# Start order, early weights, rope on VectorE, turns between blocks, and tiles at multiples of 512 bytes in a hybrid S5 and attention layer

## The chip, the core and the metric

One core of a Trainium2 chip runs the whole layer. The core has five engines with queues of their own: TensorE (PE, matrix products and transposes), VectorE (DVE), ScalarE (ACT), GpSimd (POOL) and SyncE (SP, which here only issues DMAs). The metric is the device time of one execution in microseconds. All times below are of this core.

## The reference, cut to what matters

512 tokens of width 1024 pass one decoder layer. One projection of the normalised input feeds an S5 branch, a dilated attention branch and two gates.

```python
h = rms_norm(x, norm_w)
proj = h @ w_in
u_s, z_s, q, k, v, z_a, r_s, r_a = split(proj)

# S5 branch: diagonal complex state space in 4 chunks of 128 tokens
y_s = s5_branch(u_s, lam_re, lam_im, log_dt, b_re, b_im, c_re, c_im, d_skip, w_glu)
y_s = (y_s * silu(z_s)) @ w_ssm_out

# attention: 3 head groups (dilation 1, 4, 16), 8 heads of 64, window of 129 keys
q, k = rms_norm(q, q_norm_w), rms_norm(k, k_norm_w)
q, k = apply_partial_rope(q, positions), apply_partial_rope(k, positions)   # first 16 of 64
y_a = dilated_attention(q, k, v)     # softmax per group, groups merged by their sums
y_a = (y_a * silu(z_a)) @ w_attn_out

m = sigmoid(r_s) * y_s + sigmoid(r_a) * y_a
out = x + m @ w_o
```

All of it is float32. In `s5_branch` the complex recurrence `h[t] = a * h[t-1] + B u[t]` runs over 64 groups with 64 states, then `Re(C h) + D u`, GELU and a gated product with `w_glu`.

## The kernel before, in words

**Products.** Each large product is done as three products of a reduced float32 type: an operand is split in a high part (`hi`) and what is left (`lo`), and `hi*hi + lo*hi + hi*lo` is summed (`mm3`, line 63 is the helper that records every matmul, line 67 the one that records every transpose). So each weight tile of 128 x 1024 numbers is loaded by SP into `w_raw` (two buffers), its high part is made by ACT (`w_hi`, L116) and its low part by DVE (`w_lo`, L118); for the first two weights by POOL, since `lo_w` holds `pool` at the start. There are three buffers each of `w_hi` and `w_lo`, and weights are fetched two ahead of their use (`look`).

**Order.** The program is written as one stream of stages; a scheduler with a model of the engines sets the order of each engine's queue. `tc.issue_after(ins)` makes what is written inside it stand behind the instruction `ins` on its engine. Between the stages, units of the large projection are put as fillers.

**Stages.** (1) x comes in four blocks of 128 tokens (`x_t[0..3]`, tile `x_all`); ACT sums the squares (L240), DVE works out the reciprocal root by integer and Newton steps (L123 to L128, L242), DVE and ACT scale a block each (L248, L246), TensorE transposes (`hps`), ACT and DVE make `hT_hi` (L259) and `hT_lo` (L260). This is done in two halves of 256 tokens. (2) Eight u units (`u_unit`): the first three by halves, so that they begin when the first half of hT is there; each one's result `uT` goes to DRAM and comes back in another layout (`ud`, `sza`, `uss`). Beside them DVE works out the tables of S5 (L348 to L417 and L460 to L463) and rope's sine and cosine. (3) `W` and `xps` (inputs of the scan; the coefficients come from `coef`, L285 to L287), then the scan itself on DVE (L647 to L652, written into `Xs`), with projection units as fillers on TensorE. (4) y units (`yps`), GELU, the gated product, the output of the S5 branch. (5) Four attention blocks `hp = 0..3` of two heads per group.

**An attention block.** `qk_first` and `qk_second` project q, k and v with tokens on partitions ("TOK" products: 128 x 512, weights high and low against hT). `qk_norm` scales them (L858) and applies rope on POOL (L864 to L869: four operations on the first 16 of each 64 columns of `qraw`). `qk_turn` transposes them (`qtp`) and copies them with the norm weights as a factor (`wcol`; ACT L885, DVE L886) into `qkp`. The scores go to `sps`, DVE masks them (L941), ACT takes the exponential into `Pt` (L943), DVE and POOL work out the merged denominators (L978 to L986, sums per token moved by POOL in `sfb`, L990) and DVE scales `Pt` (L997). `values` transposes `Pt` (`ptp`), copies it (`ptb`; ACT L1039, DVE L1041) and multiplies by `V` into `ot`. A block's values are computed within the next block's projection, ahead of the last of `qk_second`'s four weights (`mid`, with `kq == 3`), and the scheduler may move them; `v0_unit` projects the V of group 0 with a bank of the pool `pj`.

Of the kernel before, what the change touches and what calls it, by code (L numbers as in the profile page):

```python
# [13 lines left out]
I32 = mybir.dt.int32  # L14
# [38 lines left out]
def tile_hybrid_block(ctx: ExitStack, tc: tile.TileContext, x, positions, norm_w, w_in, lam_re, lam_im,  # L53
# [83 lines left out]
    lo_w = [dve]  # L137
# [55 lines left out]
    def load_w(srcs, kts, cols):  # L193
        raw = wp.tile([P, kts, cols], F32, name="w_raw", tag="w_raw", bufs=2)
        w = cols // len(srcs)
        for i, s in enumerate(srcs):
            sp.dma_start(raw[:, :, i * w:(i + 1) * w], s.rearrange("(k p) c -> p k c", p=P))
# [39 lines left out]
    junk = big.tile([P, D], F32, name="junk", tag="s6a")  # L237
    for h in range(2):
        for r in (2 * h, 2 * h + 1):
            act.activation(junk, x_t[r], AF.Square, accum_out=ss[:, r:r + 1])  # L240
# [3 lines left out]
        for r in (2 * h, 2 * h + 1):  # L244
            if r % 2:
                act.activation(x_t[r], x_t[r], AF.Copy, scale=rst[:, r:r + 1])  # L246
            else:
                dve.tensor_scalar(x_t[r], x_t[r], rst[:, r:r + 1], None, op0=ALU.mult)  # L248
        for q in range(KT // 2):
# [18 lines left out]
    Xs = big.tile([P, 2, G // 2, NI, NJ], F32, name="Xs", tag="s2")  # L268
    Xsv = Xs.rearrange("p a g i j -> p a g (i j)")

    def load_u(j, Uj=None):
# [3 lines left out]
        return Uj.rearrange("p (g c) -> p g c", g=8)  # L275

    def coef(dst, p0, a1, a2, n0, n1, t, eng):
# [9 lines left out]
        dve.tensor_tensor(dst, dst, tv, op=ALU.add)  # L287
# [37 lines left out]

    first = [(get_w(), pj_tile()) for _ in range(3)]
# [7 lines left out]
    lr = scr([G, N])  # L334
    li = scr([G, N])
    dt = scr([G, 1])
    sp.dma_start(lr, lam_re[0])
    sp.dma_start(li, lam_im[0])
    sp.dma_start(dt, log_dt.rearrange("o g -> g o"))
# [36 lines left out]
    dte = scr([G, 1])  # L376
    exp_exact(dte, dt, [G, 1], "ea")
# [86 lines left out]
    act.activation(BB[:, 0], BB[:, 2], AF.Copy, scale=-1.0)  # L464

# [9 lines left out]
    for j in range(3, 8):  # L475
        u_unit(j)
        for i in {3: (0, 1, 2), 4: (3,)}.get(j, ()):
            early[i] = load_u(i, sza[:, i])
# [73 lines left out]
    qkw = scr([P, 2, NG, HD])  # L552
    sp.dma_start(qkw[:, 0].rearrange("p g d -> p (g d)"),
                 q_norm_w[0].rearrange("g d -> (g d)").unsqueeze(0).to_broadcast([P, NG * HD]))
    sp.dma_start(qkw[:, 1].rearrange("p g d -> p (g d)"),
                 k_norm_w[0].rearrange("g d -> (g d)").unsqueeze(0).to_broadcast([P, NG * HD]))
    dve.tensor_scalar(qkw[:, 0], qkw[:, 0], -0.125, None, op0=ALU.mult)
    wps = bank("wcp")
    for g in range(NG):
        for a in range(2):  # L560
            wd = sml.tile([1, 2, HD], F32, name="wd", bufs=2)
            pool.tensor_copy(wd, qkw[0:1, a, g].unsqueeze(1).broadcast_to([1, 2, HD]))
            pe.matmul(wps[:, 2 * g + a:2 * g + a + 1], wd.rearrange("p a d -> p (a d)"), ident[0:1, 0:1],
                      start=True, stop=True, skip_group_check=True)
    dve.tensor_copy(wcol.rearrange("p g a -> p (g a)"), wps[:, 0:6])
    pool.memset(wcol[0:16], 1.0)
    pool.memset(wcol[64:80], 1.0)

    tC = cst.tile([P, NG, NB, 2, 16], F32, name="tC")
    tS = cst.tile([P, NG, NB, 2, 16], F32, name="tS")  # L570
    for g in range(NG):
        for a in range(2):
# [618 lines left out]
```

## Time and profile before

| | |
|---|---|
| median of 3 runs | 720.77 us (719.61 to 723.12) |
| profiled execution | 722.95 us |
| its span (first to last instruction) | 721.2 us |
| TensorE busy | 689.3 us (96%), 4789 instructions |
| DVE busy | 460.8 us (64%) |
| ACT busy | 314.8 us (44%) |
| POOL busy | 179.8 us (25%) |
| DMA | 82.14 MB, 114 GB/s mean |

A row of the waits names the engine and line that stood idle, what released it, the total, the number of times and the longest. A row of the timeline gives start, duration, engine, line, operation, what it writes and reads, its shape, and in brackets the idle time before it with what ended it. A row of the stretches gives each engine's busy time (and count) in a stretch, then the granted clock of TensorE as a share of full speed, the share of DMA time and GB/s.

### The profile page before, as it was taken

How to read it: one execution, taken by the hardware profiler on the slowest of the kernel's cores; microseconds unless marked ns; L12 is line 12 of the kernel's file. 1: busy time of each engine (PE TensorE's matmuls, PEld its weight loads, DVE VectorE, ACT ScalarE, POOL GpSimd, SP SyncE). 2: the span in 40 equal slices, each digit the busy share in tenths (PEclk: the TensorE clock that was granted, in tenths of full speed). 3: DMA queues.
4: the chain of work that ended last, by engine and by line, in shares of the span. 5: the costliest groups of instructions: out<-in, count | busy, mean ns of one | idle time of the engine just before them, and what ended most of it. 6: DMA issues, size and time to landing. Idle time of an engine off the chain costs nothing.

```text
span 721.2 us, 12599 instructions
## 1 busy us (share of the span) xinstructions
PE 689.3 (96%) x4789; PEld 571.6 (79%) x4789; DVE 460.8 (64%) x928; ACT 314.8 (44%) x631; POOL 179.8 (25%) x330
## 2 busy tenths in 40 slices
PE   2799899999999999999999999999989998999997
PEld 2697677788977888888889888788868887888886
DVE  6766865999969544674325659756764667364832
ACT  6433544423247653342144456537253734543320
POOL 3421020630316502640000326121601251220000
PEclk9989999999999999999999999999999999999999
DMA  8425742564537635555333432312312221327341
GB/s 206 107 62 149 181 108 66 131 165 153 118 86 157 150 90 161 153 163 181 104 89 100 132 88 61 87 50 69 97 50 71 77 88 30 117 75 252 128 145 59
DMA packets 137213, 82.14 MB, mean 114 GB/s; under 512 B 32696, under 2 KB 125632, under 8 KB 137024
## 3 DMA queue, kind: packets, MB, share of 16 engines
q1 hardware_dynamic: 135088, 78.96, 38.0%
q0 software_dynamic: 2048, 2.36, 2.3%
q8 instruction: 38, 0.62, 0.4%
q14 instruction: 23, 0.19, 0.1%
q10 hardware_dynamic: 16, 0.00, 0.0%
HBM read 68.46 MB, written 10.49 MB: 109 GB/s over the span
## 4 chain that ended last, share of the span: by engine, by line
PE 87%; ACT 4%; DMA 4%; SPq 2%; DVE 2%; issue 0%; ACTq 0%
PE pj L63 72%; DMA w_raw<-in_w_in_dram 4%; PE yps L63 3%; PE sps L63 3%; PE ot L63 2%; PE ptp L67 2%; PE xps L63 1%; PE kps L63 1%; ACT w_hi L116 1%; PE qtp L67 1%; SPq L454 1%; PE wps L67 1%; ACT qkp L885 1%; PE yT L67 1%; SPq L227 1%; ACT ptb L1039 1%
## 5 line engine op out<-in xcount | busy, mean ns | idle before, releaser
L116 ACT ACTIVATE w_hi<-w_raw 128x1024 fp32r<-128x1024 f32 x100 | 106.2, 1063 | 230.2 <-PE pj L63 196.7
L118 DVE TENSOR_TENSOR w_lo<-w_raw,w_hi 128x1024 fp32r<-128x1024 f32 x98 | 124.4, 1269 | 102.0 <-ACT w_hi L116 97.2
L63 PE MATMUL pj<-hT_lo,w_hi 128*128 128x512 f32 (+1 forms) x344 | 132.2, 385 | 3.6 <-DVE hT_lo L260 3.6
L63 PE MATMUL pj<-hT_hi,w_hi 128*128 128x512 f32 (+1 forms) x344 | 132.9, 389 | 2.7 <-ACT V L917 1.4
L63 PE MATMUL pj<-hT_hi,w_lo 128*128 128x512 f32 (+1 forms) x344 | 131.6, 384 | 1.6 <-DVE w_lo L118 1.6
L63 PE MATMUL pj<-w_hi,hT_hi 128*128 128x512 f32 (+1 forms) x288 | 106.5, 370 | 0.0
L63 PE MATMUL pj<-w_lo,hT_hi 128*128 128x512 f32 (+1 forms) x288 | 105.7, 367 | 0.0
L63 PE MATMUL pj<-w_hi,hT_lo 128*128 128x512 f32 (+1 forms) x288 | 105.3, 369 | 0.0
L63 PEld LDWEIGHTS pj<-hT_lo,w_hi 128*128 128x128 f32 x344 | 66.7, 194 | 16.0 <-DVE hT_lo L260 4.6
L63 PEld LDWEIGHTS pj<-hT_hi,w_hi 128*128 128x128 f32 x344 | 66.1, 193 | 15.4 <-ACT V L917 2.1
L63 PEld LDWEIGHTS pj<-hT_hi,w_lo 128*128 128x128 f32 x344 | 66.5, 193 | 14.5 <-DVE w_lo L118 2.7
L63 PEld LDWEIGHTS pj<-w_hi,hT_hi 128*128 128x128 f32 x288 | 54.4, 189 | 8.6 <-DVE Xs L651 0.2
L63 PEld LDWEIGHTS pj<-w_hi,hT_lo 128*128 128x128 f32 x288 | 54.4, 189 | 8.5
L63 PEld LDWEIGHTS pj<-w_lo,hT_hi 128*128 128x128 f32 x288 | 54.4, 189 | 8.4
L886 DVE SCALAR_TENSOR_TENSOR qkp<-qtp,wcol,qkp 128x512 fp32r<-128x512 f32 (+1 forms) x32 | 23.2, 747 | 26.9 <-ACT qkp L885 26.4
L943 ACT ACTIVATE Pt<-Pt,st 128x256 f32<-128x256 f32 (+1 forms) x64 | 31.0, 493 | 14.1 <-DVE st L941 14.0
L747 POOL TENSOR_TENSOR kt<-kt,dg 16x128 f32<-16x128 f32 x8 | 12.0, 1505 | 92.0 <-ACT kt L746 86.0
L864 POOL TENSOR_TENSOR rt<-qraw,tC 128x256 f32<-128x256 f32 x12 | 14.0, 1170 | 84.0 <-DVE qraw L858 83.7
L751 POOL DMA_DIRECT2D dd<-kt x64 | 33.7, 535 | 2.4 <-POOL kt L747 2.4
L885 ACT ACTIVATE qkp<-qtp,wcol 128x512 fp32r<-128x512 f32 (+1 forms) x32 | 21.2, 688 | 21.8 <-PE qtp L67 16.1
L973 POOL COPY sw<-st 32x4 f32<-32x4 f32 x64 | 11.9, 187 | 69.8 <-ACT Pt L943 67.0
L990 POOL COPY sfb<-sd 32x2 f32<-32x2 f32 x64 | 18.0, 282 | 27.9 <-DVE sd L986 25.1
(265 smaller groups left out, 1271.8 us busy)
## 6 DMA issues: line engine op xcount, KB each, us to landing
w_raw<-in_w_in_dram SPq DMA_DIRECT2D x40, 512.0 KB
w_raw<-in_w_in_dram SPq DMA_DIRECT2D x112, 128.0 KB
w_raw<-in_w_glu_dram SPq DMA_DIRECT2D x8, 512.0 KB
w_raw<-in_w_ssm_out_dram SPq DMA_DIRECT2D x8, 512.0 KB
w_raw<-in_w_o_dram SPq DMA_DIRECT2D x8, 512.0 KB
x_all<-in_x_dram SPq DMA_DIRECT2D x4, 512.0 KB
ud<-uT SPq DMA_DIRECT2D x8, 256.0 KB
uss<-ud SPq DMA_DIRECT2D x8, 256.0 KB
```

Of the source, the lines that this page charges most:

```text
L63: last[0] = nc.tensor.matmul(*a, **k)
L67: last[0] = nc.tensor.transpose(*a, **k)
L116: act.activation(hi, src, AF.Copy, scale=scale)
L118: e.tensor_tensor(lo, src, hi.bitcast(F32), op=ALU.subtract)
L747: pool.tensor_tensor(kt[:, :, T - 1, :], kt[:, :, T - 1, :], dg, op=ALU.add)
L751: pool.dma_start(M[Q * t:Q * t + Q, :, 0:P - Q * t], kt[:, :, t:].rearrange("q g k p -> q g (k p)"))
L864: pool.tensor_tensor(t1, rh[:, :, :, 0:16], cv.broadcast_to([P, NB * 2, 2, 16]), op=ALU.mult)
L885: act.activation(hi, ps[sl], AF.Copy, scale=w)
L886: dve.scalar_tensor_tensor(lo, ps[sl], w, hi.bitcast(F32), op0=ALU.mult, op1=ALU.subtract)
L943: act.activation(o, o, AF.Exp, bias=nm, scale=-1.0, accum_out=st[:, kind, 1, h, b:b + 1])
L973: pool.tensor_copy(sw[32 * r:32 * r + 32, :, :, b], st[32 * b:32 * b + 32, 1, :, :, r])
L990: pool.tensor_copy(fb[32 * b:32 * b + 32, :, r], d[32 * r:32 * r + 32, 1, :, b])
```

## The change: what it does

- **Tiles at multiples of 512 bytes.** A tile `room` of 320 bytes per partition goes in ahead of `hT_hi`; the large tiles began at 192 modulo 512, now they begin at 0. The small `wd` tiles are gone (below).
- **First low parts on DVE.** `load_w` is split in `fetch_w` (the DMA) and the split into parts; DVE makes all low parts.
- **ScalarE's order at the start is fixed** by `last_act`: Square 0 and 1, `w_hi` of weight 0, Square 2, scaling, seven `hT_hi`, `w_hi` of weight 1, the eighth, `w_hi` of weight 2, Square 3, and so on. The three small DMAs of lambda and dt go to ACT's queue, at the start.
- **Weights into Xs.** `w_early` holds four weights in the region in which `Xs` is set up later (behind the fourth u unit). Weights 2 to 5 are fetched there right behind x; weights 6 and 7 go to the two raw buffers.
- **Tables behind hT.** S5's table work on DVE stands behind the second half's scaling and hT (`behind_h`); the scan's tables behind the coefficients; rope's tables behind the W units. `wcol` comes from one transpose instead of six small products.
- **Rope on DVE** for all groups of all blocks.
- **Turns between blocks of six products**: the four turns of a block's first two groups are put one each ahead of four token blocks of `qk_second` and tied there. `values` is put behind the token block (2, 1) of the weights for `hp == 0`, behind (1, 3) else. All `ptb` copies are ACT's, except in the last block. The V of group 0 gets a bank of its own (`v0p`).

```diff
+    room = cst.tile([P, 80], F32, name="room")
+    pool.memset(room[:, 0:1], 0.0)
...
-    def load_w(srcs, kts, cols):
-        raw = wp.tile([P, kts, cols], F32, name="w_raw", tag="w_raw", bufs=2)
+    def fetch_w(i, raw=None):
+        srcs, kts, cols = plan[i]
+        if raw is None:
+            raw = wp.tile([P, kts, cols], F32, name="w_raw", tag="w_raw", bufs=2)
...
+    def load_w(i, hi_behind=None, lo_behind=None):
+        if i not in raws_in:
+            fetch_w(i)
+        raw = raws_in.pop(i)
...
-        split(hi, lo, raw, lo_eng=lo_w[0])
+        with queued_after(hi_behind):
+            last_act[0] = act.activation(hi, raw, AF.Copy).ins
+        with queued_after(lo_behind):
+            dve.tensor_tensor(lo, raw, hi.bitcast(F32), op=ALU.subtract)
...
-    lo_w[0] = pool
+    w_early = big.tile([P, 4, KT, P], F32, name="w_early", tag="s2")
     for r in range(NB):
         sp.dma_start(x_t[r], xv[r])
         if r in (1, 2):
-            prefetch(len(loaded) + 1)
-    lo_w[0] = dve
+            fetch_w(r - 1)
+    fetch_w(2, w_early[:, 0])
...
+        if h:
+            loaded.append(load_w(2, last_act[0], lo_done))
+            square(3)
...
+        if h == 0:
+            loaded.append(load_w(0, last_act[0], scaled))
+            square(2)
...
+            if h == 0 and q == 2:
+                loaded.append(load_w(1, hi_done, lo_done))
...
+    for i in range(3):
+        fetch_w(3 + i, w_early[:, 1 + i])
     first = [(get_w(), pj_tile()) for _ in range(3)]
...
+    behind_h = ExitStack()
+    behind_h.enter_context(tc.issue_after(scaled))
+    behind_h.enter_context(tc.issue_after(hi_done))
...
+    def tables_last():
+        with tc.issue_after(coefs[0]):
+            scan_tables()
...
+    with tc.issue_after(coefs[0]):
+        pos_i = scr([P, NB], I32)
...
+        pe.transpose(wps[:, 0:2 * NG], wq, ident[:2 * NG, :2 * NG])
...
-            pool.tensor_tensor(t1, rh[:, :, :, 0:16], cv.broadcast_to([P, NB * 2, 2, 16]), op=ALU.mult)
+            dve.tensor_tensor(t1, rh[:, :, :, 0:16], cv.broadcast_to([P, NB * 2, 2, 16]), op=ALU.mult)
...
-                    if h == 0:
+                    if h == 0 or hp < NP - 1:
                         act.copy(pt[:, k0 * P:], ps[:, k0 * P:])
...
-            def mid(kq):
-                if kq == 1:
-                    qk_turn(0, raws[0], *QK)
-                if kq == 2:
-                    with queued():
-                        qk_turn(1, raws[1], *QK)
-                if kq == 3:
-                    values(hp, Pt, V)
+            steps = {(2, 3): (0, 0), (3, 0): (0, 1), (3, 1): (1, 0), (3, 2): (1, 1)}
+
+            def mid(kq, r):
+                if (kq, r) not in steps:
+                    return False
+                g, a = steps[kq, r]
+                with queued():
+                    qk_turn(g, raws[g], *QK, turned=(a,))
+                return True
+
+            def after(kq, r):
+                if (kq, r) == ((2, 1) if hp == 0 else (1, 3)):
+                    values(hp, Pt, V)
...
-            finv = v0_unit(hp + 1, V)
+            finv = v0_unit(hp + 1, V, bank("v0p"))
```

ACT's queue at the start, before (`junk` is the output of Square, `x_all` a scaling, `hT_hi` a high part of h, the `L371` and `L372` rows are of the tables):

```order
3 L240 ACTIVATE junk,scr<-x_all 128x1024 x2
4 L116 ACTIVATE w_hi<-w_raw 128x1024
5 L240 ACTIVATE junk,scr<-x_all 128x1024
6 L246 ACTIVATE x_all<-x_all,scr 128x1024
7 L116 ACTIVATE w_hi<-w_raw 128x1024
8 L240 ACTIVATE junk,scr<-x_all 128x1024
9 L259 ACTIVATE hT_hi<-hps,nwc 128x256 x8
10 L116 ACTIVATE w_hi<-w_raw 128x1024
11 L246 ACTIVATE x_all<-x_all,scr 128x1024
12 L371 ACT_TABLE_LOAD
13 L371 ACTIVATE scr<-scr 128x32
14 L372 ACTIVATE scr<-scr 128x32
```

The second weight's high part and the fourth Square stand ahead of the first `hT_hi`, and a table load with two sines ahead of the second half's. Now:

```order
7 L215 ACTIVATE w_hi<-w_raw 128x1024
8 L266 ACTIVATE junk,scr<-x_all 128x1024
9 L283 ACTIVATE x_all<-x_all,scr 128x1024
10 L294 ACTIVATE hT_hi<-hps,nwc 128x256 x7
11 L215 ACTIVATE w_hi<-w_raw 128x1024
12 L294 ACTIVATE hT_hi<-hps,nwc 128x256
13 L215 ACTIVATE w_hi<-w_early 128x1024
14 L266 ACTIVATE junk,scr<-x_all 128x1024
15 L283 ACTIVATE x_all<-x_all,scr 128x1024
16 L294 ACTIVATE hT_hi<-hps,nwc 128x256 x8
17 L215 ACTIVATE w_hi<-w_early 128x1024
18 L331 COPY uT<-pj 128x4x8x8x2
```

Seven of the first half's pieces come right behind the scaling, the second weight behind the seventh; the third weight is in `w_early`, and the tables' work stands behind the first `uT`.

TensorE's queue in the projection of block 2, where the values of block 1 are computed, before (`pj` is the TOK product, `ptp` a transpose of `Pt`, `ot` the product with V, `qtp` a turn):

```order
2025 L67 MATMUL qtp<-ident,qraw 128x128 x4
2026 L63 MATMUL pj<-w_hi,hT_lo 128x512
2027 L63 MATMUL pj<-w_hi,hT_hi 128x512
2028 L63 MATMUL pj<-w_lo,hT_hi 128x512
2029 L63 MATMUL pj<-w_hi,hT_lo 128x512
2030 L67 MATMUL qtp<-ident,qraw 128x128 x4
2031 L67 MATMUL ptp<-ident,Pt 128x128 x10
2032 L63 MATMUL ot<-ptb,V 64x4x32 x6
2033 L67 MATMUL ptp<-ident,Pt 128x128 x20
2034 L63 MATMUL ot<-ptb,V 64x4x32 x8
2035 L63 MATMUL ot<-ptb,V 64x128 x16
```

All 30 transposes and 30 products with V stand together at the end of the projection. Now:

```order
2006 L63 MATMUL pj<-w_hi,hT_lo 128x512
2007 L67 MATMUL ptp<-ident,Pt 128x128 x4
2008 L63 MATMUL ot<-ptb,V 64x4x32 x6
2009 L67 MATMUL ptp<-ident,Pt 128x128 x8
2010 L63 MATMUL ot<-ptb,V 64x4x32 x8
2011 L67 MATMUL ptp<-ident,Pt 128x128 x8
2012 L63 MATMUL ot<-ptb,V 64x128 x8
2013 L67 MATMUL qtp<-ident,qraw 128x4x32 x4
2014 L63 MATMUL pj<-w_hi,hT_hi 128x512
2015 L63 MATMUL pj<-w_lo,hT_hi 128x512
2016 L63 MATMUL pj<-w_hi,hT_lo 128x512
```

Ten transposes stand 18 products ahead of the first row (46 behind the scores), the rest alternate with the products with V, and turns of four come behind, with six TOK products between two of them.

The same place for block 0's values, now (before, the first six `ptp` stood 62 TOK products behind the scores):

```order
1763 L63 MATMUL pj<-w_hi,hT_lo 128x512
1764 L67 MATMUL ptp<-ident,Pt 128x128 x8
1765 L63 MATMUL ot<-ptb,V 64x4x32
1766 L67 MATMUL ptp<-ident,Pt 128x128 x8
1767 L63 MATMUL ot<-ptb,V 64x4x32 x5
1768 L67 MATMUL ptp<-ident,Pt 128x128 x2
1769 L63 MATMUL ot<-ptb,V 64x4x32
1770 L67 MATMUL ptp<-ident,Pt 128x128 x4
1771 L63 MATMUL ot<-ptb,V 64x4x32 x7
1772 L67 MATMUL ptp<-ident,Pt 128x128 x8
1773 L63 MATMUL ot<-ptb,V 64x128 x8
1774 L67 MATMUL qtp<-ident,qraw 128x4x32 x4
```

Twenty-one TOK products stand between the last scores and the first of these transposes, and no TOK product stands among them.

More of the change, by code (lines that the diff above doesn't have):

```diff
@@ L1 @@
 import math
-from contextlib import ExitStack
+from contextlib import ExitStack, nullcontext
 import numpy as np
@@ L237, in tile_hybrid_block, with square @@
     junk = big.tile([P, D], F32, name="junk", tag="s6a")
+    def square(r):
+        with queued_after(last_act[0]):
+            last_act[0] = act.activation(junk, x_t[r], AF.Square, accum_out=ss[:, r:r + 1]).ins
+    square(0)
+    square(1)
     for h in range(2):
-        for r in (2 * h, 2 * h + 1):
-            act.activation(junk, x_t[r], AF.Square, accum_out=ss[:, r:r + 1])
+        if h:
+            loaded.append(load_w(2, last_act[0], lo_done))
+            square(3)
         w = slice(2 * h, 2 * h + 2)
@@ L243, in tile_hybrid_block @@
         rsqrt(rst[:, w], ms[:, w], [P, 2], ra_[:, w], rb_[:, w])
[L244 to L248, printed above, removed]
+        scaled = dve.tensor_scalar(x_t[2 * h], x_t[2 * h], rst[:, 2 * h:2 * h + 1], None, op0=ALU.mult).ins
+        if h == 0:
+            loaded.append(load_w(0, last_act[0], scaled))
+            square(2)
+        with queued_after(last_act[0]):
+            r = 2 * h + 1
+            act.activation(x_t[r], x_t[r], AF.Copy, scale=rst[:, r:r + 1])
         for q in range(KT // 2):
@@ L333, in tile_hybrid_block @@
         u_unit(j, first[j][1])
[L334 to L339, printed above, removed]
+    for j in range(3):
+        early[j] = load_u(j, sza[:, j])
     def exp_exact(dst, src, shape, pfx):
@@ L476, in tile_hybrid_block @@
         u_unit(j)
[L477 to L478 removed]
+        if j == 3:
+            Xs = big.tile([P, 2, G // 2, NI, NJ], F32, name="Xs", tag="s2")
+            Xsv = Xs.rearrange("p a g i j -> p a g (i j)")
+        if j == 4:
+            early[3] = load_u(3, sza[:, 3])
         wx(*((), (), (0,), (1,), (2, 3))[j - 3])
@@ L549, in tile_hybrid_block @@
     maskB_f = maskB.rearrange("p a k -> p (a k)")
[L552 to L572, printed above, removed]
-            w1 = qkw[:, a, g, 0:8].unsqueeze(1).broadcast_to([P, NB, 8])
-            w2 = qkw[:, a, g, 8:16].unsqueeze(1).broadcast_to([P, NB, 8])
-            pool.tensor_tensor(tC[:, g, :, a, 0:8], rcos, w1, op=ALU.mult)
-            pool.tensor_tensor(tC[:, g, :, a, 8:16], rcos, w2, op=ALU.mult)
-            pool.tensor_tensor(tS[:, g, :, a, 0:8], rsin, w2, op=ALU.mult)
-            pool.tensor_tensor(tS[:, g, :, a, 8:16], rsin, w1, op=ALU.mult)
-    pool.tensor_scalar(tS[:, :, :, :, 0:8], tS[:, :, :, :, 0:8], -1.0, None, op0=ALU.mult)
     def tok_granule():
@@ L594, in tok_granule, with v0_unit @@
         return pss
-    def v0_unit(hp, V):
-        ps = cm_unit(hT_hi, hT_lo)
+    def v0_unit(hp, V, ps=None):
+        ps = cm_unit(hT_hi, hT_lo, ps=ps)
         vt = t2k("vt")
@@ L906, in qk_first, with qk_second @@
         return raws
-    def qk_second(hp, mid=None):
-        pss = wide_granule(hT_hi, hT_lo, mid)
+    def qk_second(hp, mid, after):
+        pss = wide_granule(hT_hi, hT_lo, mid, after)
         raw = new_raw(0)
```

111 lines of the change are left out of this document (75 added, 36 removed).

## The prediction

> **What bounds the kernel now.** The page's busy times come first, then the waits of TensorE, then its busy time by stretch.
>
> ```profile
> PE 689.3 (96%) x4789; PEld 571.6 (79%) x4789; DVE 460.8 (64%) x928; ACT 314.8 (44%) x631; POOL 179.8 (25%) x330
> ```
> ```profile
> PE hps L67 <- DVE x_all L248: 10.2, 1, 10.2
> PE ptp L67 <- ACT ptb L1039: 3.5, 6, 0.8
> PE xps L63 <- ACT W L307: 3.1, 1, 3.1
> ```
> ```profile
> 0.00:18.00 18.00, 5.22 (x25) 4.86 (x25) 11.60 (x45) 11.14 (x18) 6.87 (x13) 1.00 0.87 206
> 18.00:36.00 18.00, 13.02 (x96) 11.58 (x95) 14.20 (x74) 8.60 (x18) 7.96 (x29) 0.96 0.43 108
> 36.00:54.00 18.00, 18.00 (x158) 16.48 (x158) 10.93 (x31) 5.51 (x7) 3.92 (x2) 0.85 0.27 61
> 54.00:72.00 18.00, 16.64 (x74) 12.67 (x73) 12.23 (x23) 5.68 (x7) 3.07 (x4) 1.00 0.57 148
> 72.00:90.00 18.00, 14.76 (x124) 12.18 (x123) 14.95 (x31) 10.46 (x21) 0.00 (x0) 0.91 0.71 182
> 90.00:126.00 36.00, 36.00 (x350) 28.02 (x350) 22.51 (x34) 15.73 (x45) 5.35 (x7) 1.00 0.32 87
> 126.00:200.00 74.00, 74.00 (x499) 61.83 (x498) 69.36 (x100) 25.43 (x43) 25.03 (x30) 1.00 0.53 139
> ...
> 440.00:455.00 15.00, 15.00 (x79) 12.33 (x78) 14.40 (x39) 7.45 (x17) 10.74 (x24) 1.00 0.24 70
> 512.00:540.00 28.00, 25.53 (x175) 20.84 (x174) 18.16 (x30) 12.29 (x25) 8.71 (x9) 1.00 0.27 76
> ```
>
> Columns behind the stretch: its length, then busy time of PE, weight loads, DVE, ACT and POOL, the granted clock, DMA share, GB/s. TensorE is the bound, 689.3 us of a span of 721.2, so a saving counts only if it removes matmul time or fills one of its 32 us of holes. Of these 22.7 lie before 90 us (12.8, 5.0, 1.4 and 3.2 by the rows), about 2.5 in each of two attention blocks, and the tail after 702 us is not touched. To them comes the lower clock of 0.96, 0.85 and 0.91, which stretches matmuls without showing as a hole: 18 x (0.04 + 0.15 + 0.09) = 5.0 us. DVE is full beside a full TensorE in 126 to 200 (the scan) and in 440 to 455 (the first block's softmax): work added there can become a wait.
>
> **Start: low parts on DVE, ScalarE's order, four weights fetched early.**
>
> ```profile
> 9.07 2.34 POOL L118 TENSOR_TENSOR w_lo<-w_raw,w_hi 128x1024 fp32r<-128x1024 f32 x1 [6.37 <-ACT w_hi L116]
> ...
> 8.99 0.16 DVE L128 SCALAR_TENSOR_TENSOR scr<-scr 128x2 f32<-128x2 f32 x1
> 9.19 2.23 DVE L126 TENSOR_TENSOR scr<-scr 128x2 f32<-128x2 f32 x1
> 11.85 0.75 DVE L248 TENSOR_SCALAR x_all<-x_all,scr 128x1024 f32<-128x1024 f32 x1
> ...
> 9.31 1.06 ACT L240 ACTIVATE junk<-x_all 128x1024 f32<-128x1024 f32 x1 [0.32 <-DMA x_all<-in_x_dram]
> 11.85 1.15 ACT L246 ACTIVATE x_all<-x_all,scr 128x1024 f32<-128x1024 f32 x1 [1.40 <-DVE scr L128]
> 23.54 1.06 ACT L116 ACTIVATE w_hi<-w_raw 128x1024 fp32r<-128x1024 f32 x1 [3.98 <-DMA w_raw<-in_w_in_dram]
> 26.75 1.15 ACT L246 ACTIVATE x_all<-x_all,scr 128x1024 f32<-128x1024 f32 x1 [2.16 <-DVE scr L128]
> ...
> 12.66 3.67 PE L67 MATMUL hps<-ident,x_all 128*128 128x128 f32 x16 [10.15 <-DVE x_all L248]
> 15.99 0.77 PE L63 MATMUL pj<-hT_hi,w_hi 128*128 128x256 f32 x2
> ```
>
> The reciprocal root's tiny steps take 0.16 us each, but the one that starts at 9.19 takes 2.23: it ends with the POOL subtraction that began at 9.07. With the low part on DVE, behind the scaling of x0, it costs 0.2, so x0 is scaled from 9.8 (11.85 less 2.05). ScalarE scales x1 after its third Square (9.31 + 1.2), 10.5 to 11.6. The transposes that need x1 run from 11.6 instead of 13.0, and with 16 at 0.22 us the first product starts at about 14.8 instead of 15.99.
>
> "SBUF — State Buffer" in the Trainium skill (section "SBUF: two separate sides") calls the port pair of VectorE and GpSimd an exclusive lock: a VectorE operation with two SBUF inputs blocks fully against a GpSimd operation that reads SBUF. By that rule, the trace agrees: 2.23 us for a step of 0.16. [...]
>
> The first half's 72 products of 256 columns then take 8.6 us at 0.12 (the rows on the pace below), with one more for a clock not yet up (an allowance): end 24.7. The third weight, whose high part came at 23.54 because its DMA waited for a raw buffer, now lies in the region of Xs behind x3, and is split right after the first hT (about 17 to 19), before its unit is due at 20.6. The second half's x was scaled at 26.75, because DVE and ScalarE had let S5's table work run between; in the new order fourth Square, root (12 x 0.2) and scaling follow by 22.6, so transposes come right behind the first half, hT's eight pieces pace until 29, and 72 products end near 36.0.
>
> ```profile
> 45.33 0.28 PE L63 MATMUL pj<-hT_hi,w_lo 128*128 128x256 f32 x1
> ```
>
> It was 45.3, part of it the clock of 0.85, which came behind the holes of 24 to 36. Term: **-9.3**, from -7.3 (the clock falls again) to -10.6.
>
> **45 to 90 us: weights held by two raw buffers, ScalarE queued behind them.**
>
> ```profile
> 65.92 1.06 ACT L116 ACTIVATE w_hi<-w_raw 128x1024 fp32r<-128x1024 f32 x1 [5.63 <-DMA w_raw<-in_w_in_dram]
> 75.07 1.06 ACT L116 ACTIVATE w_hi<-w_raw 128x1024 fp32r<-128x1024 f32 x1 [5.50 <-DMA w_raw<-in_w_in_dram]
> 76.88 1.11 ACT L307 COPY W<-wps 128x512 f32<-128x512 f32 x2
> ```
>
> ScalarE stood 5.5 us and more at a high part whose DMA was late; behind it in its queue are the copies of uT and of W, and for W TensorE waited the 3.1 us above. With weights 2 to 5 already there, and 6 and 7 in the raw buffers, the eight u units never wait for a load. The stretch 54 to 90 holds 4.6 us of holes and 18 x 0.09 = 1.6 of clock: 6.2. Against it: S5's table work on DVE now starts behind the second half's hT, near 24 instead of 13, and W needs its result. Some 20 us of such small operations plus four low parts end near 52, and the first W is asked for after the sixth unit, near 53. Two more table loads of ScalarE lie under matmuls. I take 1.6 us of new waits (from 0 to 4, the next stall of the old size). Term: **-4.6**, from -2 to -6.2.
>
> **Scan and tables.** Rope's tables leave the start for the end of the W units.
>
> ```profile
> 29.52 0.24 POOL L577 TENSOR_TENSOR tS<-scr 128x32 f32<-128x32 f32 x1 [3.37 <-ACT scr L371]
> ...
> 198.18 0.69 DVE L652 TENSOR_TENSOR Xs<-Xs,scn 128x512 f32<-128x512 f32 x1
> ...
> 204.11 1.10 PE L63 MATMUL yps<-ab,Xs 64*64 64x64 f32 x60
> ```
>
> DVE finished the scan 5.2 us before TensorE read Xs (198.18 + 0.69 against 204.11). A dozen coefficient steps now stand ahead of the scan instead of between its steps, which adds nothing; new ahead of Xs are some 38 small steps of rope's and the scan's tables at 0.16 to 0.2, 6 to 8 us, and POOL's 24 table products (0.24 us each, the first in the rows) can each hold a DVE step up, 6 more: 6 to 14. The order gives TensorE 65 instead of 19 products between the last other work and that read, 46 x 0.228 = 10.5 us more cover. With 5.2 + 10.5 of cover against them: **0**, from 0 to +3 (a unit behind it that waits for its coefficients).
>
> **Attention: values among the TOK products, rope on DVE.**
>
> ```profile
> 500.25 1.32 PE L63 MATMUL sps<-qkp 64*128 64x256 f32 x12
> ...
> 527.29 0.66 PE L67 MATMUL ptp<-ident,Pt 128*128 128x128 f32 x4 [0.78 <-ACT ptb L1039]
> 536.12 0.50 PE L63 MATMUL pj<-hT_hi,w_hi 128*128 128x512 f32 x1 [0.46 <-ACT V L917]
> ...
> 506.62 2.06 DVE L997 TENSOR_SCALAR Pt<-Pt,sd 128x128 f32<-128x128 f32 x8
> ...
> 506.86 5.08 POOL L990 COPY sfb<-sd 32x2 f32<-32x2 f32 x15
> ```
> ```profile
> L416 DVE TENSOR_TENSOR pw<-pw,tq x3: 210/274/409, 38.0 to 44.7; 64x64 f32<-64x64 f32 x1, 64x128 f32<-64x128 f32 x1, 64x256 f32<-64x256 f32 x1
> ```
>
> Blocks 1 and 2 lose 2.5 us each where 30 transposes of Pt wait for ScalarE's copies. The change splits them by 46 and 18 products and by the value products; Pt, ready 7.2 us after the scores' last (501.5, then 508.7 to 512.6), is asked for 46 x 0.228 = 10.5 us after them, so it is there. I take the 2.5 and 0.3 of slower pitch beside them: -2.8 each, from -1.5 to -3.4. Block 0 has 21 products ahead, 4.8 us. Its first Pt is there after about 6.8 and the part behind the sfb copies after 11.3 (506.86 + 5.08 + 0.8 against 501.5), with only 6.5 us of its own work between: a stall of about 3.5, less the 0.6 it loses today: +2.9, from 0 to +6. Rope by the row above: 0.41 + 0.27 + 0.27 + 0.41 = 1.4 us a group (1.1 by spacing), 12 groups, 13 to 17 us of DVE. Its turns come 22 us behind the scores and rope ends by about 18: nothing on TensorE's path, except in block 0, where one group stands in DVE's queue ahead of the softmax; that is the +6. Term: -2.8 - 2.8 + 2.9 = **-2.7**, from -7 to +3.
>
> **Tiles at multiples of 512 bytes.**
>
> ```profile
> 20.06 0.28 PE L63 MATMUL pj<-hT_hi,w_hi 128*128 128x256 f32 x1
> 23.06 0.28 PE L63 MATMUL pj<-hT_lo,w_hi 128*128 128x256 f32 x1
> ...
> 451.15 0.40 PE L63 MATMUL pj<-w_hi,hT_hi 128*128 128x512 f32 x1
> 456.85 0.39 PE L63 MATMUL pj<-w_lo,hT_hi 128*128 128x512 f32 x1
> ```
>
> Between the first two rows lie 25 starts, 0.120 us each; between the other two 25, 0.228 each. So 256 more columns cost 0.108 and each matmul a fixed 0.012. All operands began at 192 modulo 512, in both directions, so the trace shows no other case. The fixed part may be the matmul's own (it is the same for 1 KB and 2 KB rows and for both operand orders): **0**; if all of it came from the starts, about 2,100 matmuls would give back 2,100 x 0.012 = 25 us.
>
> "TensorE: Matmul & The Clock Gate" in the skill (section "Wait — 56ns, not 53.3ns?") measures start-to-start 215.7 ns for 512 columns of warm matmuls; the trace's 228 is 12 above. By the page's gap the sum would be 25 us lower, as in the first rival; whether the 12 come from the data type or the starts no run here shows.
>
> **Sum.** -9.3 - 4.6 + 0 - 2.7 + 0 = -16.6 on the profiled execution of 722.95 us (span 721.2 and 1.75 around it): 706.4. That execution is 2.2 above the median of 720.77, so I expect a median of **704 us**. The terms' ends add to -24 and -3; not all fall to one side, so the case's own range is 695 to 715.
>
> **Rivals.** (1) The starts set the matmul's fixed part: 704 - 25 = **679**. For it: the fixed part is in every row, and an operand at 192 touches one 512-byte piece more than it needs at either size; against: any cost of starting a matmul would look the same, and no row singles the address out. Chance 0.14. (2) The start gains, but attention loses in all blocks, because DVE, with rope, delivers Pt late: 440 to 455 is full already. Block 0 at +6, the others at 0, scan +3, tables +2: 704 + 3.1 + 5.6 + 3 + 2.4 = **718**. Chance 0.10. (3) Slower: the scan's chain on DVE becomes the bound. It is 74 us long and 94% busy; if it cannot start at the last W unit but only after the tables (14 us) and the dozen coefficient steps in series (0.69 and up by the row of Xs, 8 us), Xs comes 22 us later, of which 15.7 is cover. The cover's 46 products, and 20 more that the order puts elsewhere (129 instead of 149 between the y units), are then missing as fillers there, 66 x 0.228 = 15 us: 704 + 6.3 + 15 = **725**. It decides once DVE's added work passes the 15.7 us. Against it stand the holes DVE has before 126 (36 less 22.5 busy). Chance 0.08. (4) The early fetch does not do what it says, because all four early weights share the queue with x3 and delay it: the start gains only the 2 us of the lock, 704 + 7 = 711, inside the range; chance 0.06, from the forecast's share of 0.68.
>
> **Chances.** A measurement here tells about 0.5% (3.6 us) from no change. Forecast 0.68 with (4), all faster; (1) faster; of (2) two thirds within 0.5%, the rest faster; (3) slower: faster 0.85, same 0.07, slower 0.08. The range takes in the terms' ends, (2), and a part of (1), where only some matmuls gain: 686 to 718.
>
> **What would show it.** Right: the wait of hps shrinks to about 8.5 us with no 2 us root step; no w_hi wait for w_raw over 2 us before 90; products of the second half end near 36; clock near 1.00 from 30 on; ptp's waits for ptb nearly gone in blocks 1 and 2 and 3 us of waits for Pt in block 0; 512-column pace 0.228. Wrong: a pace near 0.216, a hole ahead of yps, or Pt late in blocks 1 and 2.

## The result and the profile after

The changed kernel takes 702.21 us (median of 6, 701.93 to 702.40) against 720.93 us for the kernel before in the same comparison: a ratio of 0.9734, 95% interval 0.9719 to 0.9748, or 18.7 us less. Its profiled execution took 702.34 us (span 700.4), 20.6 us below the 722.95 of before, which lay 2.2 above its own median. The forecast was 704.

The waits of TensorE in the changed kernel (engine and line, what released it, total, times, longest), and the busy time by stretch:

```profile
PE hps L67 <- DVE x_all L277: 8.2, 1, 8.2
PE nps L67 <- DMA nw<-in_norm_w_dram: 2.3, 1, 2.3
PE pj L63 <- DVE hT_lo L295: 0.2, 1, 0.2
```
```profile
0.00:18.00 18.00, 7.48 (x41) 6.80 (x41) 10.24 (x33) 11.58 (x19) 2.20 (x12) 1.00 0.92 291
18.00:36.00 18.00, 17.76 (x141) 16.86 (x140) 14.80 (x68) 9.11 (x17) 0.94 (x2) 1.00 0.63 112
36.00:54.00 18.00, 18.00 (x138) 14.12 (x137) 14.97 (x39) 9.48 (x14) 6.51 (x6) 1.00 0.53 126
54.00:72.00 18.00, 18.00 (x149) 15.09 (x148) 18.00 (x29) 9.46 (x16) 0.22 (x1) 1.00 0.63 169
72.00:90.00 18.00, 18.00 (x173) 14.74 (x172) 14.25 (x22) 10.22 (x27) 0.96 (x1) 1.00 0.46 115
...
670.00:702.00 32.00, 26.74 (x118) 21.80 (x117) 9.03 (x11) 2.81 (x3) 0.00 (x0) 0.99 0.23 83
```

Nothing is left in the list but the start; the 3 us of waits for Pt that were forecast for block 0 are not there either. Every stretch between 18 us and the tail is full to within 0.24 us, and the clock stands at 1.00 in all of them: the lower clock of 0.85 to 0.96 went with the holes. The page's chain of waits is 97% TensorE, where it was 87%.

Where the time came from is read by laying the same product of both traces side by side; their last products lie 20.5 us apart. The last product of the u units' second half started at 45.33 and now starts at 35.41; the first product of the gated stage at 279.66 and now 260.09; the last of all at 716.82 and now 696.35. So the start gave 9.9 us, the work from there to the gated stage 9.7, the gated stage and everything behind it 0.9. Three rows of the changed kernel mark the start:

```profile
9.91 0.75 DVE L277 TENSOR_SCALAR x_all<-x_all,scr 128x1024 f32<-128x1024 f32 x1
...
14.14 0.56 PE L63 MATMUL pj<-hT_hi,w_hi 128*128 128x256 f32 x1
...
35.41 0.28 PE L63 MATMUL pj<-hT_hi,w_lo 128*128 128x256 f32 x1
```

x0 is scaled at 9.91 instead of 11.85, the first product starts at 14.14 instead of 15.99. In the scan TensorE waits for nothing:

```profile
188.96 0.69 DVE L653 TENSOR_TENSOR Xs<-Xs,scn 128x512 f32<-128x512 f32 x1
...
195.26 0.93 PE L63 MATMUL yps<-ab,Xs 64*64 64x64 f32 x48
```

Xs is complete 5.6 us before TensorE reads it, against 5.2 before.

### The profile page after: what moved, and what is told of

Its sections match the earlier page's. It is cut to its first block, busy times and chain, and to the rows that moved or that the text cites. A ratio compares the mean times of both kernels' runs of the same rounds, so it can differ in the third digit from the quotient of the medians.

```text
span 700.4 us, 12561 instructions
## 1 busy us (share of the span) xinstructions
PE 686.0 (98%) x4778; PEld 567.9 (81%) x4778; DVE 461.1 (66%) x967; ACT 322.4 (46%) x645; POOL 120.9 (17%) x275
## 4 chain that ended last, share of the span: by engine, by line
PE 97%; DVE 1%; DMA 1%; ACT 0%; issue 0%; SPq 0%; ACTq 0%
PE pj L63 77%; PE sps L63 3%; PE yps L63 3%; PE ot L63 2%; PE v0p L63 2%; PE ptp L67 2%; PE qtp L67 2%; PE xps L63 1%; PE kps L63 1%; PE wps L67 1%; DMA x_all<-in_x_dram 1%; PE yT L67 1%; DVE hT_lo L295 1%; PE hps L67 1%; PE cps L63 0%; PE atp L63 0%
## 5 line engine op out<-in xcount | busy, mean ns | idle before, releaser
L217 DVE TENSOR_TENSOR w_lo<-w_raw,w_hi 128x1024 fp32r<-128x1024 f32 x96 | 118.1, 1231 | 78.3 <-ACT w_hi L215 76.5
L63 PE MATMUL pj<-hT_hi,w_hi 128*128 128x512 f32 (+1 forms) x320 | 121.2, 381 | 0.0
L63 PE MATMUL pj<-hT_lo,w_hi 128*128 128x512 f32 (+1 forms) x320 | 120.9, 379 | 0.2 <-DVE hT_lo L295 0.2
L63 PE MATMUL pj<-hT_hi,w_lo 128*128 128x512 f32 (+1 forms) x320 | 120.6, 378 | 0.0
L63 PEld LDWEIGHTS pj<-hT_lo,w_hi 128*128 128x128 f32 x320 | 60.4, 189 | 11.4 <-DVE hT_lo L295 0.7
L63 PEld LDWEIGHTS pj<-hT_hi,w_lo 128*128 128x128 f32 x320 | 60.3, 189 | 11.0 <-DVE w_lo L217 0.2
L63 PEld LDWEIGHTS pj<-hT_hi,w_hi 128*128 128x128 f32 x320 | 60.1, 189 | 10.8 <-ACT hT_hi L294 0.3
L63 PEld LDWEIGHTS sps<-qkp 128*128 128x128 f32 (+1 forms) x192 | 23.2, 187 | 4.3 <-issue 1.5
L63 PE MATMUL sps<-qkp 128*128 128x256 f32 (+2 forms) x192 | 25.6, 287 | 0.0
L63 PE MATMUL pj<-yT_hi,w_hi 128*128 128x512 f32 x64 | 24.9, 389 | 0.0
```

The lines of the kernel that those rows point to most:

```text
L63: last[0] = nc.tensor.matmul(*a, **k)
L217: dve.tensor_tensor(lo, raw, hi.bitcast(F32), op=ALU.subtract)
```

## The experiments

Each takes one part of the change out, or puts one part alone into the kernel before. Medians are set against 702.2 us for the changed kernel, which came out at 702.21 and, in a later comparison beside three of these kernels, at 702.16.

**1. Without the shift to multiples of 512 bytes**

```diff
-    room = cst.tile([P, 80], F32, name="room")
-    pool.memset(room[:, 0:1], 0.0)
```

> The changed kernel without the 320-byte tile: hT, weights and most other tiles begin at 192 modulo 512 again, all else is the same. Theory (the start address costs TensorE nothing, the gain comes from holes): 702.2 within 0.7, 512-column pace 0.227 as before and after. Rival (addresses matter, for the products or for the weight DMAs): over 704, at the most 702 + 25 = 727, with a pace that differs from 0.227 or with weights landing later.

702.25 us. The same run of 128 x 512 products, first and last of 20 (19 distances), in the changed kernel and without the shift:

```profile
427.34 0.40 PE L63 MATMUL pj<-w_lo,hT_hi 128*128 128x512 f32 x1
...
431.71 0.39 PE L63 MATMUL pj<-w_hi,hT_lo 128*128 128x512 f32 x1
```
```profile
427.21 0.40 PE L63 MATMUL pj<-w_lo,hT_hi 128*128 128x512 f32 x1
...
431.57 0.39 PE L63 MATMUL pj<-w_hi,hT_lo 128*128 128x512 f32 x1
```

0.230 and 0.229 us each. The start address costs neither the products nor the loads anything that shows here; the 0.012 us fixed part of a product is not the address.

**2. Attention: places and rope, two by two**

Three kernels fill the square: rope on POOL with the new places, the old places with rope on DVE, and both as before.

```diff
-            dve.tensor_tensor(t1, rh[:, :, :, 0:16], cv.broadcast_to([P, NB * 2, 2, 16]), op=ALU.mult)
+            pool.tensor_tensor(t1, rh[:, :, :, 0:16], cv.broadcast_to([P, NB * 2, 2, 16]), op=ALU.mult)
```

> The changed kernel with rope's four operations a group back on POOL. Theory (rope is off TensorE's path, its turns come over 20 us behind the scores): 702.2 to 703.5, the extra being block 0, where POOL's sfb copies stand behind rope again. Rival (POOL's rope blocks DVE by the shared port, or delivers late): 2 to 4 us more in each of three blocks, 708 to 714.

```diff
+                if kq == 1:
+                    qk_turn(0, raws[0], *QK)
+                if kq == 2:
+                    with queued():
+                        qk_turn(1, raws[1], *QK)
+                if kq == 3:
+                    values(hp, Pt, V)
...
-            finv = v0_unit(hp + 1, V, bank("v0p"))
+            finv = v0_unit(hp + 1, V)
...
-                    if h == 0 or hp < NP - 1:
+                    if h == 0:
```

> The changed kernel with the attention order of before: turns of a whole group ahead of weights 1 and 2, values ahead of weight 3, low heads' ptb copies on DVE, V of group 0 in a pj bank; rope stays on DVE. Theory (blocks 1 and 2 gained 1.8 and 2.4 in the trace, block 0 lost 2.0): plus 2 to 3 us, 704 to 705. Rival A (the new places cost as much as they give): 702.2 within 0.7. Rival B (they carry a large part of the 18.7 us): 707 or more.

Both edits together:

> The changed kernel with the attention order of before and with rope back on POOL, so that only the front of the kernel is changed. Theory (rope on DVE is what makes the old order slow; new places and DVE rope hang together): the attention part takes what it took in the kernel before, about 1 us more than in the changed kernel, 702.7 to 704. Rival (the places alone carry the 8 us that the old places cost with rope on DVE): 708 to 711.

| us | rope on DVE | rope on POOL |
|---|---|---|
| new places | 702.2 | 702.9 |
| old places | 710.3 | 703.3 |

With the new places it makes under 1 us which engine does rope, and with rope on POOL about as little where turns and values stand; both came out in the range expected. The four runs with new places and rope on POOL split, though: 702.02, 702.16, 703.70 and 703.76. The 703.70 is the profiled one. In it TensorE waits 1.9 us for a copy of the transposed Pt in the last block and 0.4 us for Pt in each of blocks 1 and 2, but not in block 0, where I had expected the extra. Only the old places with rope on DVE cost, 8 us: my expectation for that kernel (704 to 705) was wrong and rival B held. The waits of TensorE in it, and then in the kernel with both as before:

```profile
PE ptp L67 <- ACT ptb L1086: 5.2, 4, 2.1
...
PE pj L63 <- ACT V L964: 1.4, 3, 0.5
PE ptp L67 <- DVE ptb L1088: 1.2, 3, 0.7
PE qtp L67 <- DVE qkp L933: 0.5, 2, 0.2
```
```profile
PE ptp L67 <- ACT ptb L1086: 3.5, 6, 0.8
...
PE pj L63 <- ACT V L964: 1.4, 3, 0.5
PE ptp L67 <- DVE qkp L933: 0.6, 2, 0.3
```

The longest single wait grows from 0.8 to 2.1 us, and it stands at the copies of Pt, not at rope. ScalarE's rows ahead of that copy, with old places and rope on DVE:

```profile
507.93 1.20 ACT L962 COPY qraw<-pj 128x256 f32<-128x256 f32 x4
508.97 1.11 ACT L215 ACTIVATE w_hi<-w_raw 128x1024 fp32r<-128x1024 f32 x1
509.93 1.26 ACT L932 ACTIVATE qkp<-qtp,wcol 128x512 fp32r<-128x512 f32 x2
511.07 0.48 ACT L1086 COPY ptb<-ptp 128x384 f32<-128x384 f32 x1
```

The transposes of Pt started at 508.96, and the first copy, 0.48 us long, starts 2.1 us later, behind four copies, a weight's high part and two copies of a turn. With rope on POOL the same copy starts 1.6 us behind its transposes, with one turn's copy ahead of it in place of two. These waits are only a part: the two traces differ by 6.4 us from the first gated product to the last of all (443.6 against 437.2), and the rows above by 2.8. Another 1.1 us is lost from step to step among the first block's scores, in the traces with rope on DVE at the old and at the new places, and in neither with rope on POOL. The rest lies in other steps too short for the list. Whether the cause is DVE's load or only the order that the scheduler makes of it was not taken apart. What is shown is that the two edits belong together: with the old places rope on DVE costs about 7 us, with the new ones nothing that the medians show.

**3. Without the four early weights**

```diff
-    w_early = big.tile([P, 4, KT, P], F32, name="w_early", tag="s2")
-    fetch_w(2, w_early[:, 0])
-    for i in range(3):
-        fetch_w(3 + i, w_early[:, 1 + i])
```

> The changed kernel without the four early weights: weights 2 to 5 go through the two raw buffers, as before; order of ScalarE, low parts and tables stay. Theory (the early weights carry the holes of 45 to 90 us and the third weight's wait): the third unit waits 3 to 4 us in the first half, and 4 to 8 us come back between 45 and 90: 709 to 714. Rival (the queue order of ScalarE and the tables behind hT carry the gain, loads would have come in time): below 705.

711.15 us, 9 us back, inside the range but not by the parts expected: TensorE waits 4.2 us for the third weight, about as forecast, but the start loses more than this wait. The third weight's row on ScalarE, what stands behind it, and the stretch:

```profile
24.04 1.06 ACT L215 ACTIVATE w_hi<-w_raw 128x1024 fp32r<-128x1024 f32 x1 [6.71 <-DMA w_raw<-in_w_in_dram]
25.01 1.04 ACT L264 ACTIVATE junk<-x_all 128x1024 f32<-128x1024 f32 x1
...
28.82 1.15 ACT L281 ACTIVATE x_all<-x_all,scr 128x1024 f32<-128x1024 f32 x1 [2.69 <-DVE scr L128]
```
```profile
18.00:36.00 18.00, 13.53 (x83) 12.49 (x83) 9.38 (x42) 6.28 (x12) 0.87 (x2) 0.81 0.46 111
```

ScalarE waits 6.7 us for the load, and since its order is fixed, the fourth Square and the scaling of x3 wait behind it: x3 is scaled at 28.82 instead of 22.13, and the clock falls to 0.81. The last product of the second half starts at 42.57 instead of 35.41. So 7.2 us come back before 43 us and only 2.6 later. A fixed order makes the early load a condition: a late load now holds up all that stands behind it.

**4. The early weights alone, in the kernel before**

```diff
+    w_early = big.tile([P, 4, KT, P], F32, name="w_early", tag="s2")
...
+    for n in range(2, 6):
+        fetch_w(n, w_early[:, n - 2])
...
+        if j == 3:
+            Xs = big.tile([P, 2, G // 2, NI, NJ], F32, name="Xs", tag="s2")
```

> The kernel before with the four early weights alone (weights 2 to 5 fetched right behind x into the region of Xs, which is set up behind the fourth u unit); low parts on POOL, order left to the scheduler, tables and attention as before. Theory (the loads carry most of the front's gain; without them 9 us came back): 720.4 less 7 to 10, 710 to 713. Rival (they need ScalarE's fixed order and the tables behind hT): 715 or more.

717.81 us against 722.01, a ratio of 0.9945 (0.9929 to 0.9962): 4.2 us, and the rival held. The waits of TensorE:

```profile
PE hps L67 <- DVE x_all L262: 9.4, 1, 9.4
PE wcp L63 <- POOL wd L577: 3.8, 1, 3.8
```

The first transposes wait about as long as before (9.4 us), but the last product of the second half starts at 40.13 instead of 45.33: 5.2 of the 6.1 us by which this trace ends sooner than that of before are there. Behind it the early weights gave only 0.9, since the wait for W has moved to the small products with which `wcol` is made. Taking those products out too, with the one transpose:

> The kernel before with the four early weights and with the one transpose in place of the six small products. Theory (the early weights alone gave only 4.2 us, since the wait moved on: TensorE then stood 3.8 us at the small products for POOL's copies): with that wait gone 3 to 4 us more, 713.5 to 715.5. Rival (the next wait takes its place, for W or for the tables): 716.5 to 718.

716.27 us against 721.55, a ratio of 0.9925 (0.9896 to 0.9955), 5.3 us. The wait for POOL is gone, and the next has come:

```profile
PE hps L67 <- DVE x_all L262: 10.2, 1, 10.2
PE kps L63 <- DVE ab L299: 3.7, 3, 2.2
```

The value lies between what the two theories expected, nearer the rival's: the wait moved on a second time, to a coefficient on DVE. The intervals of the two ratios overlap, so a gain of this second edit over the first is not shown.

**5. Low parts of the first two weights on POOL**

```diff
-            dve.tensor_tensor(lo, raw, hi.bitcast(F32), op=ALU.subtract)
+            (pool if i < 2 else dve).tensor_tensor(lo, raw, hi.bitcast(F32), op=ALU.subtract)
```

> The changed kernel with the low parts of the first two weights on POOL again. Theory (a VectorE step of the reciprocal root is blocked beside each): x0 is scaled 2 us later and the first half starts 1 to 2 us later; plus 1 to 3 us, 703.2 to 705.2, with one root step over 2 us. Rival (DVE is freed of 2.4 us and the hT chain hides the step): 702.2 within 0.7.

705.00 us, 2.8 more, as expected in size, but not by the step that I expected. The rows:

```profile
9.77 0.75 DVE L277 TENSOR_SCALAR x_all<-x_all,scr 128x1024 f32<-128x1024 f32 x1
...
18.40 2.21 DVE L217 TENSOR_TENSOR w_lo<-w_early,w_hi 128x1024 fp32r<-128x1024 f32 x1 [0.47 <-ACT w_hi L215]
```
```profile
10.11 2.64 POOL L217 TENSOR_TENSOR w_lo<-w_raw,w_hi 128x1024 fp32r<-128x1024 f32 x1 [7.37 <-ACT w_hi L215]
17.13 2.40 POOL L217 TENSOR_TENSOR w_lo<-w_raw,w_hi 128x1024 fp32r<-128x1024 f32 x1 [4.38 <-ACT w_hi L215]
```

The root is through at 9.77, before POOL begins, so no step of it is blocked. It is the second one: beside it DVE's own low part takes 2.21 us where it takes 1.22 alone, TensorE waits 0.7 us for POOL's, and the second half's products end 0.9 us later. The profiled execution took 704.22 us; another 0.9 of it comes between 36 and 101 us, where no wait is listed but TensorE changes more often between W's transposes and the scan's inputs (11 times instead of 6). The rest up to the median of 705.00 is in no trace.

**6. S5's tables free to run ahead of hT**

```diff
-    behind_h.enter_context(tc.issue_after(scaled))
-    behind_h.enter_context(tc.issue_after(hi_done))
```

> The changed kernel without the rule that holds S5's table work behind the second half's hT. By the order of the queues a table load of 1.28 us and two sines now stand ahead of the first hT on ScalarE, and the small steps among DVE's hT work. Theory (both halves' hT come later, the tables were not late): plus 1.5 to 5 us, 703.7 to 707. Rival (tables finished earlier let W start earlier and pay it back): 702.2 within 0.7.

707.41 us, 5.2 more, just above the theory's range. On ScalarE:

```profile
13.02 1.15 ACT L283 ACTIVATE x_all<-x_all,scr 128x1024 f32<-128x1024 f32 x1 [2.10 <-DVE scr L128]
14.19 1.28 ACT L406 ACT_TABLE_LOAD   x1
...
16.41 2.79 ACT L294 ACTIVATE hT_hi<-hps,nwc 128x256 fp32r<-128x256 f32 x7 [0.52 <-PE hps L67]
```

x1 is scaled at 13.02 instead of 11.33, since DVE's small table steps stand among those of the root, and hT begins at 16.41 instead of 13.24. The last product of the second half starts at 42.07, 6.7 us later. The first `xps` starts only 3.4 us later, but that is a matter of order and pays nothing back: TensorE waits 2.0 us for W there, and the first gated product is 7.6 us later (267.69 against 260.09), as is the last product of all. This profiled execution took 710.03 us, the other three 707.2 to 707.6; what they lost less is in no trace.

**7. The six small products, at the new place**

```diff
-        pe.transpose(wps[:, 0:2 * NG], wq, ident[:2 * NG, :2 * NG])
+                pe.matmul(wps[:, 2 * g + a:2 * g + a + 1], wd.rearrange("p a d -> p (a d)"), ident[0:1, 0:1],
+                          start=True, stop=True, skip_group_check=True)
```

> The changed kernel with the norm weights' column made by six small products from POOL copies again, at the new place. Theory (in the trace before, the steps into, among and out of these products and two others took 2.0 us over their streaming on TensorE, which no term of the sum had): plus 1 to 2 us, 703.2 to 704.2. Rival (they cost only where POOL's copies are late, at the old place): 702.2 within 0.6.

704.19 us against 702.16 in the same comparison: 2.0 us, as expected; 1.5 of it stands in the two traces at the first gated product. The rows of TensorE with the products, then with the transpose:

```profile
98.98 0.60 PE L63 MATMUL wcp<-ident,wd 1*128 1x1 f32 x4
99.51 0.50 PE L63 MATMUL pj<-hT_hi,w_hi 128*128 128x512 f32 x1
...
109.09 0.38 PE L63 MATMUL wcp<-ident,wd 1*128 1x1 f32 x2
109.40 0.50 PE L63 MATMUL pj<-hT_hi,w_hi 128*128 128x512 f32 x1
```
```profile
99.10 0.22 PE L67 MATMUL wcp<-ident,scr 6*128 6x6 f32 x1
99.25 0.50 PE L63 MATMUL pj<-hT_hi,w_hi 128*128 128x512 f32 x1
```

Two of the small products (four records) hold TensorE 0.53 us, from 98.98 to 99.51, the transpose 0.15. That is no wait, so no list of waits names it.

**8. A version meant to be faster**

```diff
             loaded.append(load_w(0, last_act[0], scaled))
-            square(2)
...
             loaded.append(load_w(2, last_act[0], lo_done))
+            square(2)
             square(3)
```

> A version meant to beat both: the changed kernel with the third block's Square taken from between the first weight's high part and the scaling of x1 on ScalarE, and put next to the fourth block's Square. Theory (the transposes wait for x1, which waits for that Square; TensorE is the bound from there on, so a shift of the start stays): x1 is scaled from about 10.0 instead of 11.3, the first product starts near 13.0 instead of 14.1, and the end moves by 0.8 to 1.4: 700.8 to 701.4. Rival (the second half's root comes later by that Square, and the first half's end waits for it): 702.2 within 0.4.

Beside it, on the same chip:

> The changed kernel unchanged, beside the version above on the same chip: 702.2 within 0.4 by all theories.

703.28 us (703.24 to 703.41) against 702.16 (702.09 to 702.27): slower by 1.1, and both theories fell. The rows of ScalarE and TensorE:

```profile
9.90 1.15 ACT L283 ACTIVATE x_all<-x_all,scr 128x1024 f32<-128x1024 f32 x1
13.07 2.79 ACT L294 ACTIVATE hT_hi<-hps,nwc 128x256 fp32r<-128x256 f32 x7 [2.03 <-PE hps L67]
...
61.27 1.06 ACT L215 ACTIVATE w_hi<-w_raw 128x1024 fp32r<-128x1024 f32 x1 [3.39 <-DMA w_raw<-in_w_in_dram]
```
```profile
10.64 3.67 PE L67 MATMUL hps<-ident,x_all 128*128 128x128 f32 x16 [7.46 <-DVE x_all L278]
```

x1 is scaled at 9.90 instead of 11.00 in the changed kernel beside it, and nothing else moves. The sixteen transposes take 3.3 us with either x1, and the first product stands behind all of them (13.97 here, 13.88 in the changed kernel beside it). Record by record, the first eight are those of x0 and the ninth is the first that waits for ScalarE's x1; it starts at 12.41 here and at 12.32 there, when x1 had been ready since 11.05 and 12.13. The 35.28 and 35.24 at which the second half's last product starts are the same. The loss comes later, between 36 and 101 us: the scheduler made another order from there on, in which ScalarE waits 3.39 us for a load and `xps` starts 1.7 us later. No wait of TensorE is listed for it; the 1.1 us lie in small steps, half of them at four more changes between W's transposes and the scan's inputs. None of these kernels beats the changed one.

## Why the prediction was right, step by step

The total was right: -16.6 us forecast on the profiled execution, -20.6 measured; 704 against 702.2 for the median. Of the five terms three held, one was half of what it measured, one was three times too large. That the total came nearer than these two is luck: one gave 5.1 us more than forecast, the other 1.8 less.

- **Start, -9.3: measured -9.9.** The second half was to end near 36.0 and ends at 35.41, the first half near 24.7 and ends at 24.02. x0's scaling at 9.8 (9.91) and the third weight's wait held too. One reason in it was wrong: "the transposes that need x1 run from 11.6". The transposes of x0 run from 10.7 and those of x1 behind them, from 12.5, and experiment 8 shows that the start hangs on x0 and on sixteen transposes in a row at 0.21 us. So the first product came at 14.14 and not at 14.8. The price for the blocked root step held for the kernel before, where the step took 2.23 us; in the fixed order the same POOL work does its harm at another place (experiment 5).
- **45 to 90 us, -4.6: measured -9.7 up to the gated stage.** This is the mis-sized term, outside its own range of -2 to -6.2. (The 22.7 us of holes before 90 us that the prediction names at its start are 22.4 by its own four rows; no term uses the sum.) The 6.2 us of holes and clock went entirely, and the 1.6 us of new waits that I set against them never came: no stretch from 36 to 90 us has a hole. The step that failed is the list of what the change removes: the six small products were read as a matter of POOL and of no weight, and they cost TensorE 2.0 us (experiment 7). The 1.5 us that remain to 9.7 were not taken apart.
- **Scan, 0: held.** 6 to 14 us of added work were set against 15.7 us of cover; the margin that is left is 5.6 us, and TensorE does not wait. Rival (3), DVE as the bound, is out.
- **Attention, -2.7: measured -0.9 for everything behind 260 us.** The blocks are compared by what TensorE loses from start to start beyond the columns' own time (0.00042 us a column, from 0.227 and 0.120 us for 512 and 256), from a block's last scores to the next block's last. Block 1 goes from 11.1 to 9.2 us and block 2 from 10.7 to 8.5, so -1.9 and -2.3 where I had -2.8 each: the waits for `ptb` are gone, as forecast. Block 0 goes from 8.1 to 10.3, +2.1 where I had +2.9, but not by the stall for Pt that the term was made of. (Its 3.5 us did not follow from its own figures either: 6.8 less 4.8 is 2.0, and 4.8 and 6.5 make the 11.3 at which the rest is there.) The first Pt is scaled at 431.75, 5.0 us behind the scores' last, its transposes start at 432.09, and no wait is listed:

```profile
432.09 1.33 PE L67 MATMUL ptp<-ident,Pt 128*128 128x128 f32 x8
433.36 0.43 PE L63 MATMUL ot<-ptb,V 128*64 128x128 f32 x2
433.72 1.16 PE L67 MATMUL ptp<-ident,Pt 128*128 128x128 f32 x8
434.82 0.87 PE L63 MATMUL ot<-ptb,V 128*64 128x128 f32 x10
```

  The step that failed here is one that the sum put at nothing: the change of kind. From the last transpose of a row of them to the next product with V it takes 0.20 us, where the next transpose follows after 0.11; and 0.20 us back, where the next product with V follows after 0.06. The new places make 33 such changes in the four blocks instead of 14, so some 2 us (an estimate from these steps) are given back in the blocks. The rest of the term, +1.1, is lost among block 0's own scores, and no term had it; experiment 2 finds it in both traces with rope on DVE. That rope stays off TensorE's path was right for the new places only: it was argued from the distance of 22 us to the turns, and in the old places the same operations cost 7 us (experiment 2). Rival (2) named that danger, but put it at Pt; as far as the list of waits shows it, it came at the copies of the transposed Pt.
- **Multiples of 512 bytes, 0: held.** Rival (1) at 679 us is out by experiment 1. The page "TensorE: Matmul & The Clock Gate" of the Trainium skill (section "Wait — 56ns, not 53.3ns?") has 215.7 ns from start to start for 512 columns; the runs have 229 to 230 in these rows at both addresses, so the 14 more are not the address. That they belong to the data type was not tried.
- **Rival (4)**, early loads that delay x3, is out: the second half's x was scaled at 22.1 and TensorE's waits list no load but that of the norm weights.

The parts do not add up one by one. Taken out of the changed kernel alone, the early weights cost 9.0 us, the tables' rule 5.2, the low parts 2.8, the small products 2.0: 19 us, about all that the front gave, and the fixed order, which was not tried alone, is not in that sum. Put alone into the kernel before, the early weights gave 4.2. Each of them removes one of several delays that follow one another, so what one is worth depends on which of the others are gone.

## What to carry to other kernels

Where a kernel is bound by one engine with holes, follow each hole to what is late next: here one removed wait gave way to the next twice, and the full gain came only with the whole set. An edit that looks free (rope on an engine that has time) may be free only with another one; a two-by-two of kernels tells it in three runs. And what stands on the bounding engine counts even where no wait is listed: tiny products have a price of their own, and so has each change between transposes and products with V. Work that is spread out to hide a wait is worth the wait less these changes.

## What the runs showed of the hardware that was not expected

- A product of one row and one column holds TensorE for a quarter of a microsecond: two of them, recorded as four instructions, took from 98.98 to 99.51 us before the next large product started, while a 6 x 6 transpose took 0.15.
- A change between transposes (128 x 128) and products with V (128 x 64) holds TensorE for 0.20 us from start to start, where two transposes follow after 0.11 and two such products after 0.06. It is the same in all 14 and 33 places of the kernels before and after within 0.01 us, whether or not the step waits for a semaphore.
- The high part of hT starts only 2.4 us after the first of sixteen transposes (10.64 to 13.07 in experiment 8), though its bank is written by only four of them, two of each block of x: the eight of x0 stand ahead in the queue, so the bank's last is the tenth. That one is the first that releases ScalarE, and it is through at 13.04. In the second half, with steps of 0.11 us instead of 0.21, the distance is 1.3 us (24.00 to 25.29).
- DVE's subtraction of 128 x 1024 took 2.21 us beside a POOL subtraction and 1.22 alone; it ends 1.1 us behind POOL's end at 19.53 (experiment 5). "SBUF — State Buffer" in the Trainium skill (section "SBUF: two separate sides") has it that VectorE's work with two SBUF inputs and GpSimd's that reads SBUF fully block each other; the trace agrees.
- In the changed kernel the clock stands at 1.00 in every full stretch. It fell to 0.81 in the 18 us with a hole of 4.2 us (experiment 3), and in the kernel before it was 0.85 in a full stretch (36 to 54 us) behind one with 5 us of holes, so a hole can cost clock behind it too.
